# Transformer layer on one core: whole up blocks in 512-column matmuls, h2 and x in tiles of 4 KB, and row sums issued inside the u stage

## The chip, the cores and the metric

One core of a Trainium2 chip runs the whole layer in one launch. The core has five engines with queues of their own: TensorE (matmuls; PE in the profile, its weight loads PEld), VectorE (DVE), ScalarE (ACT), GpSimd (POOL) and SyncE (SP, which issues most transfers). The metric is device time in microseconds (us), lower is better.

## The reference, cut to what matters

```python
S, D, DFF = 512, 1024, 2816          # tokens, model width, FFN width; all float32
h = rmsnorm(x, g_pre_mix)
q, k, v, g, u, sv, a_ret, a_sgu = split(h @ w_in)
y_ret = (layernorm(retention(q, k, v)) * silu(g)) @ w_ret_o      # both directions
u  = gelu(u)
sv = layernorm(gelu(sv))
mixed = einsum('gpq,bnqgc->bnpgc', w_spatial, sv_chunks) + b_spatial
y_sgu = (u * mixed) @ w_sgu_o
x  = x + rmsnorm((sigmoid(a_ret) * y_ret + sigmoid(a_sgu) * y_sgu) @ w_out, g_post_mix)
h2 = rmsnorm(x, g_pre_ffn)
hid = conv3(h2 @ w_up, conv_w) + conv_b     # depthwise, over the tokens
a, b = split(hid)
out = x + rmsnorm((gelu(a) * b) @ w_down, g_post_ffn)
```

## The kernel before

**Arithmetic.** Each float32 operand is kept as a high and a low part (`h2h`/`h2l`, `xh`/`xl`, `wh`/`wl`, in the type float32r). A product is three matmuls into the same PSUM tile: high x high, high x low, low x high. `mm3` (L217 to L220) issues the three. The operand that is loaded into the array (128x128, "weights" for TensorE) and the one that moves through it, 256 or 512 columns wide, are named in the profile after the arrow.

**Weights.** They come as 512 KB units in the order of a list. `w_get` hands out the next unit and, up to a few units ahead, has SyncE load raw tiles, ScalarE copy the high part (L79) and VectorE subtract for the low part (L86, `wl`, `wf`, `dl`).

**Products.** Many are done by a scheme of seven block products in place of eight (Strassen's kind). `Pair` does it for two output blocks of 128 features by all tokens, as seven products of 12 matmuls (L672) on halves of 256 tokens, T0 and T1: 48 matmuls in `part1`, 12 in `part2`, 24 in `part3`. A Pair's `part3` is issued later, behind the next Pair's `part1` or inside another block. Blocks that are not done in pairs are whole blocks: 8 pieces k of the model width by three matmuls each.

**Stages, in the time of the profiled span.** q and k up to 49 us; the retention's scores and states with groups of 512-column products between them (L480 to L482) up to 214; transposes of its result (L605) and the mixing's row sums (L722); u in four Pairs and the gates' first `part1`, 384 narrow matmuls, 217 to 263; the gates, with Pairs, blocks of 512 columns (`f_block`) and the spatial mixing (L745), to 430; the product with w_out (L820 to L822), the norms and the transposes of h2 (`turn`, L883), to 474; the up product to 709.7; the FFN's down product (`products` L1050, `add_whole` L1066), conversions of the result and the end.

**The up product.** 44 blocks, in pairs i of 22 that belong to one output of the gated convolution. The first 4 blocks (EARLY) go in halves of 256 tokens, interleaved with `turn`. i = 2 and 3 are 4 whole blocks; i = 4 to 19 are 8 couples, each a `Pair` on 2 blocks and 2 whole blocks, with the last Pair's `part3` issued inside a whole block; i = 20 and 21 are 4 whole blocks. `up_block` runs the 24 matmuls of T0, then what `between` gives, then those of T1. As a block is done, `conv`, `gated` and `down_forms` turn it into operands of the down product, on ScalarE and VectorE.

**Tiles.** h2 lies in tiles of 2 KB to a partition: for each half of the tokens and each two of the eight pieces k, one. `blk` is a pool of NBLK = 76 such tiles from which nearly all operands come, those of x (`xh`, `xl`, one for each k) and of the down product (`fh`, `fl`) too. The framework orders instructions by their dependences and keeps each engine's order as the code issues it; a tile is taken again when its last reader is done.

**Row sums.** `rw`, `ones` x `wst`, is one float32 product of 512 columns, which the trace shows as two passes (L722). ScalarE copies it to `rws`, which `mix` reads at L745's stage.

Of the kernel before, what the change touches and what calls it, by code (L numbers as in the profile page):

```python
# [10 lines left out]
F32 = mybir.dt.float32  # L11
F32R = mybir.dt.float32r
# [3 lines left out]
P = 128  # L16
D = 1024
S = 512
NT = S // P
KD = D // P  # L20
# [6 lines left out]
NW = 146  # L27
U0, GATE0, GATE1 = 32, 40, 72
LOOK = 4
NBLK = 76  # L30
WARM = 18
RES_OUT = 6
DOWN0 = NW - NF
DP = 9
WHOLE = NF - 2 * DP
EAGER = 7
# [11 lines left out]
def tile_block(ctx: ExitStack, tc, xT, x, wall, par, cs, wsp, bsp, gpost, gpre, gffn, out):  # L48
    nc = tc.nc
    sb = ctx.enter_context(tc.tile_pool(name="sb", bufs=1))  # L50
# [5 lines left out]
    def nm(s):  # L56
        uid[0] += 1
        return f"{s}_{uid[0]}"

    def blk(dt=F32, n="blk", shape=(P, S)):  # L60
        return sb.tile(list(shape), dt, tag="blk", bufs=NBLK, name=nm(n))

    def tmp(n="tmp", shape=(P, S)):
        return sb.tile(list(shape), F32, tag="tmp", bufs=6, name=nm(n))
# [7 lines left out]
    def ps(shape=(P, S)):  # L72
        return pp.tile(list(shape), F32, tag="ps", name=nm("ps"))

    def const(n, shape):
        return sb.tile(list(shape), F32, tag=n, bufs=1, name=n)

    def copy(o, i):
        nc.scalar.activation(out=o, in_=i, func=AF.Copy)  # L79

    def as32(t):
        return t.bitcast(F32)

    def split(hi, lo, src):
        copy(hi, src)
        nc.vector.tensor_sub(lo, src, as32(hi))  # L86
# [7 lines left out]
    i = 0  # L94
    while i < NW:
# [7 lines left out]
        elif i == UP0 + 2 * COUPLES[0][0]:  # L103
# [3 lines left out]
            i = UP0 + 2 * COUPLES[-1][1] + 2  # L107
        elif i == DOWN0:
            for _ in range(2):
                pairs = [[("q", i + j), ("t", i + j)] for j in range(DP)]  # L110
                whole = [[("blk", i + DP)], [("blk", i + DP + 1)]]
# [86 lines left out]
    def w_size(u):  # L198
        return 2 if u[0] in ("blk", "q", "t") else 1

    def w_next():
        u = units[w_pos[1]]
        w_ready[w_pos[1]] = w_unit(u)
        w_pos[1] += 1
        return w_size(u)

    def w_get(look=LOOK):

        i = w_pos[0]
        w_pos[0] += 1  # L210
        room = 2 * look + (2 if w_size(units[i]) == 2 else 0)
        n = sum(w_size(u) for u in units[i : w_pos[1]])
        while w_pos[1] < len(units) and (w_pos[1] <= i or n + w_size(units[w_pos[1]]) <= max(room, 9 if look == LOOK else 0)):
            n += w_next()
        return w_ready.pop(i)

    def mm3(o, ah, al, bh, bl, start, stop):  # L217
        nc.tensor.matmul(o, ah, bh, start=start, stop=False)  # L218
        nc.tensor.matmul(o, ah, bl, start=False, stop=False)  # L219
        nc.tensor.matmul(o, al, bh, start=False, stop=stop)  # L220
# [14 lines left out]
    def col(i):  # L235
        return part[:, i : i + 1]

    xh, xl, xg = [], [], {}

    def load_x(k):  # L240
        t = tmp("xT")
        nc.sync.dma_start(t, xT[k])
        h_, l_ = blk(F32R, "xh"), blk(F32R, "xl")
        nc.scalar.activation(out=h_, in_=t, func=AF.Copy, scale=col(PRE + k))
        xh.append(h_)
        xl.append(l_)
        return t
# [19 lines left out]
    for k in range(KD):  # L267
# [6 lines left out]
        wh, wl = w_get(1 if k < 4 else LOOK)  # L274
# [38 lines left out]
    ones = const("ones", [P, P])  # L313
    nc.gpsimd.memset(ones, 1.0)
    wst = blk(n="wst")
# [49 lines left out]
    raw = []  # L365
    for m in range(8):
        t = blk(n="qkraw")
# [8 lines left out]
    for t in range(NT):  # L376
# [4 lines left out]
            start=True,  # L381
            stop=True,
# [249 lines left out]
    for n, acc in enumerate(t_group()):  # L632
        if n < 2:
            for k in (n + 2, n + 6):
                t = tmp("xT")
# [82 lines left out]
    nc.sync.dma_start(wst, wsp)  # L718
    bst = blk(n="bst")
    nc.gpsimd.dma_start(bst, bsp.rearrange("g p -> (g p)")[None, :].to_broadcast([P, S]))  # L720
    rw = ps()
    nc.tensor.matmul(rw, ones, wst, start=True, stop=True)  # L722
    rws = blk(n="rws")
    copy(rws, rw)
    uT, late = [], None
    for j in range(KD // 2):
        p = Pair(AF.Gelu_apprx_tanh, lambda: blk(n="u"), scale=rbc)
        p.part1()
        if late:
            late.part3()  # L730
        p.part2()
        late = p
        uT += p.t
# [45 lines left out]
    for j in range(KD // 2):  # L779
        for o, t in gated_pair(ogh, ogl, late if j == 0 else None):  # L780
            b = blk(n="r")
# [14 lines left out]
    def bcast(src, n):  # L796
        t = halves(n)
        for i in range(2):
            nc.gpsimd.dma_start(t[i], src[None, i * S : (i + 1) * S].to_broadcast([P, S]))
        return t  # L800
# [32 lines left out]
    def row_scale(q):  # L833
# [7 lines left out]


    gpm, gpf = bcast(gpost, "gpm"), bcast(gpre, "gpr")
    h2h, h2l, h2r = ([[blk(dt, n) for _ in range(4)] for _ in range(2)]
                     for dt, n in ((F32R, "h2h"), (F32R, "h2l"), (F32, "h2r")))
    x1 = [[dp_.tile([P, S], F32, tag=f"x1_{t}{n}", name=f"x1_{t}{n}") for n in range(2)] for t in range(NT)]

    def norms(t, acc):
# [24 lines left out]
            zs.append(z)  # L873
        return zs

    two = "p (i n) -> p i n"

    def turn(t, zs):
        g, c = t // 2, slice((t % 2) * P, (t % 2 + 1) * P)
        for n in range(2):  # L880
            p = ps()
            for f in range(4):
                nc.tensor.transpose(p[:, f * P : (f + 1) * P], zs[n][:, f * P : (f + 1) * P], ident)  # L883
            for i in range(2):
                hi, lo, raw = (h[g][2 * n + i].rearrange(two, i=2)[:, :, c] for h in (h2h, h2l, h2r))
                pf = p[:, 2 * i * P : 2 * (i + 1) * P].rearrange(two, i=2)
                copy(hi, pf)
                copy(raw, pf)
                v.tensor_sub(lo, pf, as32(hi))  # L889

    def h2(k, t):
        f = slice((k % 2) * 256, (k % 2 + 1) * 256)
        g = t.start // 256
        return h2h[g][k // 2][:, f], h2l[g][k // 2][:, f]

    h2forms = {n: [None] * 4 for n in ("S1", "S2", "S3", "S4")}

# [17 lines left out]
    def h2_block(w, o, q):  # L915
        wh, wl = w
        for k in range(KD):
            c = slice(k * P, (k + 1) * P)
            mm3(o[:, q], wh[:, c], wl[:, c], *h2(k, q), k == 0, k == KD - 1)

    def up_block(between=None):
        w, o = w_get(), ps()
        h2_block(w, o, T0)
        if between:
            between()
        h2_block(w, o, T1)
        return o

    early_w, early_o = [], []
# [25 lines left out]
    gp, dforms = [], []  # L955
# [18 lines left out]
        gp.append(blk(n="gp"))  # L974
        v.tensor_mul(gp[-1], ca, cb)  # L975

    def two_parts(t):
        h_, l_ = blk(F32R, "fh"), blk(F32R, "fl")
        split(h_, l_, t)
        return h_, l_  # L980

    def down_forms(j):

        a, b = gp[2 * j], gp[2 * j + 1]
        first = blk(F32R, "fa")
        split(first[:, T0], first[:, T1], a[:, T0])
        s_ = blk(n="fs")
        v.tensor_sub(s_[:, T0], a[:, T1], b[:, T1])
        v.tensor_sub(s_[:, T1], s_[:, T0], a[:, T0])
        v.tensor_sub(a[:, T0], a[:, T0], a[:, T1])  # L990
        v.tensor_add(a[:, T1], b[:, T0], s_[:, T1])
        bh, bl = two_parts(b)
        sh, sl = two_parts(s_)
        th, tl = two_parts(a)
        dforms.append({
            "A11": (first[:, T0], first[:, T1]), "A12": (bh[:, T0], bl[:, T0]), "A22": (bh[:, T1], bl[:, T1]),
            "S1": (sh[:, T0], sl[:, T0]), "S2": (sh[:, T1], sl[:, T1]),
            "S3": (th[:, T0], tl[:, T0]), "S4": (th[:, T1], tl[:, T1]),
        })
# [10 lines left out]
    i = 0  # L1010
    while i < NF:
        if i in couples:
            p = Pair(None, lambda: tmp("c"), h2, h2forms)
            p.part1()
            o = [up_block()]
# [5 lines left out]
        else:  # L1021
            o = []
# [13 lines left out]
    whole = []  # L1036

    def products(m, j, steps={}):
        for n, (unit, at, act) in enumerate(UNITS):
            if n in (0, 3):  # L1040
                wh, wl = w_get()
            if j == 0:
                m[n] = ps()
            f = slice(at * 256, (at + 1) * 256)
            ah, al = dforms[j][act]
            for t in range(2):
                c = slice(t * P, (t + 1) * P)
                o = m[n][:, t * 256 : (t + 1) * 256]
                for i, (a_, w_) in enumerate(((ah, wh), (ah, wl), (al, wh))):
                    nc.tensor.matmul(  # L1050
                        o, a_[:, c], w_[:, f], start=j == t == i == 0,
                        stop=j == DP - 1 and i == 2 and n not in (M2, M3, M4), skip_group_check=True,
                    )
            steps.get(n, lambda: None)()
# [38 lines left out]
        M4: lambda: v.tensor_add(c21, m[M4], e1),  # L1093
    }
    for j in range(DP):
        if j < WHOLE:
            whole.append(two_parts(gp[2 * DP + j]))
        if j % 2 and late:
            down_forms(late.pop(0))
        products(m, j, steps if j == DP - 1 else {})  # L1100
        if j in (3, 5):
            w = w_get()
            for t in range(NT):
                add_whole(m, t, j // 2 - 1, w, j == 5)
            if j == 5:
                copy(c22, m[M8])
# [33 lines left out]
    for t in (0, 2, 1, 3):  # L1140
# [6 lines left out]
        for i, (b, e) in enumerate((((M2, e1), (M3, xx)), ((M4, uu), (M8, yy)))[t // 2]):  # L1147
            f = slice((t % 2) * 256, (t % 2 + 1) * 256)
# [134 lines left out]
```

## Time and profile before

| | |
|---|---|
| median of 3 runs | 832.83 us (831.78 to 833.0) |
| the profiled execution | 833.83 us, of which its span is 832.1 us |
| TensorE | 820.3 us busy, 5728 matmuls |
| VectorE | 660.1 us, 1076 instructions |
| ScalarE | 428.8 us, 729 instructions |
| GpSimd | 100.2 us, 104 instructions |
| granted TensorE clock, mean | 0.996 |
| DMA | 113 GB/s over the span |

The span is from the first to the last instruction that the profiler recorded; the rest of an execution's time lies around it. Busy times of engines overlap. A matmul's own time (some 279 ns at 256 columns, 391 at 512) is longer than the distance from its start to the next one's start, since several are in the array's pipeline at once.

### The profile page before, as it was taken

How to read it: one execution, taken by the hardware profiler on the slowest of the kernel's cores; microseconds unless marked ns; L12 is line 12 of the kernel's file. 1: busy time of each engine (PE TensorE's matmuls, PEld its weight loads, DVE VectorE, ACT ScalarE, POOL GpSimd, SP SyncE). 2: the span in 40 equal slices, each digit the busy share in tenths (PEclk: the TensorE clock that was granted, in tenths of full speed). 3: DMA queues.
4: the chain of work that ended last, by engine and by line, in shares of the span. 5: the costliest groups of instructions: out<-in, count | busy, mean ns of one | idle time of the engine just before them, and what ended most of it. 6: DMA issues, size and time to landing. Idle time of an engine off the chain costs nothing. (4 is left out here: it accounts for less than half of the span.)

```text
span 832.1 us, 14355 instructions
## 1 busy us (share of the span) xinstructions
PE 820.3 (99%) x5728; PEld 762.0 (92%) x5728; DVE 660.1 (79%) x1076; ACT 428.8 (52%) x729; POOL 100.2 (12%) x104
## 2 busy tenths in 40 slices
PE   9999999999999999999999999999999999999995
PEld 7888888888899999999988899999999999999995
DVE  7489898877898787767765679679899789997956
ACT  6635445545665444444444456456666566644431
POOL 0010000102221111133221201111111100000001
PEclk9999999999999999999999999999999999999998
DMA  8733222213233333233458121333333341243344
GB/s 291 245 115 102 76 77 77 76 52 100 72 98 126 102 102 102 80 98 102 130 173 330 51 76 31 109 105 92 124 96 93 116 145 35 81 136 114 103 127 153
DMA packets 29380, 93.84 MB, mean 113 GB/s; under 512 B 3392, under 2 KB 4032, under 8 KB 29312
## 3 DMA queue, kind: packets, MB, share of 16 engines
q1 hardware_dynamic: 26928, 86.85, 32.5%
q0 software_dynamic: 1520, 4.98, 1.8%
q10 hardware_dynamic: 864, 1.09, 0.4%
q8 instruction: 45, 0.74, 0.4%
q14 instruction: 23, 0.19, 0.1%
HBM read 88.71 MB, written 4.19 MB: 112 GB/s over the span
## 5 line engine op out<-in xcount | busy, mean ns | idle before, releaser
L86 DVE TENSOR_TENSOR wl<-raw,wh 128x1024 fp32r<-128x1024 f32 (+1 forms) x93 | 110.6, 1198 | 53.7 <-PE ps L672 27.3
L79 ACT ACTIVATE wf<-raw 128x512 fp32r<-128x512 f32 x140 | 85.3, 626 | 102.4 <-PE ps L219 37.5
L86 DVE TENSOR_TENSOR wf<-raw,wf 128x512 fp32r<-128x512 f32 x140 | 108.0, 787 | 26.6 <-ACT wf L79 25.7
L219 PE MATMUL ps<-h2l,wh 128*128 128x256 f32 x448 | 124.6, 279 | 0.2 <-DVE h2l L889 0.2
L218 PE MATMUL ps<-h2h,wh 128*128 128x256 f32 x448 | 123.7, 278 | 0.0
L220 PE MATMUL ps<-h2h,wl 128*128 128x256 f32 x448 | 123.7, 277 | 0.0
L672 PE MATMUL ps<-sh,wf 128*128 128x256 f32 x640 | 120.1, 277 | 0.1
L79 ACT ACTIVATE wh<-raw 128x1024 fp32r<-128x1024 f32 (+2 forms) x95 | 93.1, 990 | 36.4 <-DMA raw<-wall 12.8
L672 PEld LDWEIGHTS ps<-sh,wf 128*128 128x128 f32 x640 | 101.4, 188 | 0.8 <-DVE c L700 0.3
L672 PE MATMUL ps<-sl,wf 128*128 128x256 f32 x320 | 89.1, 278 | 0.0
L219 PEld LDWEIGHTS ps<-h2l,wh 128*128 128x128 f32 x448 | 83.9, 187 | 0.7 <-DVE h2l L889 0.7
L218 PEld LDWEIGHTS ps<-h2h,wh 128*128 128x128 f32 x448 | 83.8, 188 | 0.3 <-ACT h2h L79 0.3
L220 PEld LDWEIGHTS ps<-h2h,wl 128*128 128x128 f32 x448 | 83.9, 188 | 0.0
L480 PE MATMUL ps<-wh,xh 128*128 128x512 f32 x192 | 75.0, 391 | 0.0
L481 PE MATMUL ps<-wl,xh 128*128 128x512 f32 x192 | 74.9, 390 | 0.0
L482 PE MATMUL ps<-wh,xl 128*128 128x512 f32 x192 | 74.8, 390 | 0.0
L167 POOL TENSOR_TENSOR raw<-raw,raw 128x512 f32<-128x512 f32 x20 | 35.1, 1757 | 238.9 <-DVE raw L165 212.6
L1050 PE MATMUL ps<-dh,fh 128*128 128x256 f32 x216 | 60.9, 282 | 0.2 <-DVE yy L1085 0.2
L1050 PE MATMUL ps<-dh,fl 128*128 128x256 f32 x216 | 60.9, 282 | 0.0
L672 PEld LDWEIGHTS ps<-sl,wf 128*128 128x128 f32 x320 | 60.0, 188 | 0.3
L1050 PE MATMUL ps<-dl,fh 128*128 128x256 f32 x216 | 60.3, 279 | 0.0
L672 PE MATMUL ps<-xh,wf 128*128 128x256 f32 x288 | 54.4, 279 | 0.0
(304 smaller groups left out, 2036.4 us busy)
## 6 DMA issues: line engine op xcount, KB each, us to landing
raw<-wall SPq DMA_DIRECT2D x145, 512.0 KB, 3.5
x<-x SPq DMA_DIRECT2D x24, 256.0 KB, 5.9
xT<-xT SPq DMA_DIRECT2D x8, 256.0 KB, 5.1
x<-x POOLq DMA_DIRECT2D x8, 256.0 KB, 2.3
xT<-xT POOLq DMA_DIRECT2D x4, 256.0 KB, 4.1
out<-zg SPq DMA_DIRECT2D x4, 256.0 KB, 2.6
out<-zs ACTq DMA_DIRECT2D x3, 256.0 KB, 4.3
cs<-cs SPq DMA_DIRECT2D x2, 256.0 KB, 4.0
```

Source lines behind the costliest of these rows:

```text
L79: nc.scalar.activation(out=o, in_=i, func=AF.Copy)
L86: nc.vector.tensor_sub(lo, src, as32(hi))
L167: nc.gpsimd.tensor_tensor(out=w_raw["T2"], in0=w_raw["T1"], in1=w_raw["B22"], op=ALU.add)
L218: nc.tensor.matmul(o, ah, bh, start=start, stop=False)
L219: nc.tensor.matmul(o, ah, bl, start=False, stop=False)
L220: nc.tensor.matmul(o, al, bh, start=False, stop=stop)
L480: nc.tensor.matmul(acc[t], xh[k][:, c], wh[:, f], start=k == 0, stop=False)
L481: nc.tensor.matmul(acc[t], xh[k][:, c], wl[:, f], start=False, stop=False)
L482: nc.tensor.matmul(acc[t], xl[k][:, c], wh[:, f], start=False, stop=k == KD - 1)
L672: nc.tensor.matmul(o, w_[:, c], a_, start=first and k == n == 0, stop=k == 3 and n == 2, skip_group_check=True,)
L1050: nc.tensor.matmul(o, a_[:, c], w_[:, f], start=j == t == i == 0, stop=j == DP - 1 and i == 2 and n not in (M2, M3, M4), skip_group_check= ...
```

## The change

Three edits in one:

1. `up_block` takes both halves of the tokens in one matmul of 512 columns (24 for a block instead of 48). The moving operand is two pieces of 256 columns, 2 KB apart in the 4 KB tile. `between` stands ahead of k = 4, in the middle of the block. The early blocks stay at 256 columns.
2. `h2h` and `h2l` lie in 4 KB tiles (`two`, 8 of them) that hold both halves of the tokens for two pieces k; `xh` and `xl` take the same 8 tiles earlier, two pieces k to a tile. NBLK falls from 76 to 60. The forms of the down product from j = 7 on, and `whole[2]` and `whole[3]`, take such tiles as h2's come free; `whole.append` stands behind `down_forms`.
3. The row sums are issued in `row_sums()`, behind `part1` of the first u Pair.

```diff
-NBLK = 76
+NBLK = 60
...
+    def two(dt=F32R, n="two"):
+        return sb.tile([P, 2 * S], dt, tag="two", bufs=8, name=nm(n))
...
-        h_, l_ = blk(F32R, "xh"), blk(F32R, "xl")
+        if k % 2 == 0:
+            xp2.append((two(n="xh"), two(n="xl")))
+        h_, l_ = (a[:, k % 2 * S : (k % 2 + 1) * S] for a in xp2[-1])
...
-    rw = ps()
-    nc.tensor.matmul(rw, ones, wst, start=True, stop=True)
     rws = blk(n="rws")
-    copy(rws, rw)
+
+    def row_sums():
+        rw = ps()
+        nc.tensor.matmul(rw, ones, wst, start=True, stop=True)
+        copy(rws, rw)
+
...
         p.part1()
         if late:
             late.part3()
+        else:
+            row_sums()
         p.part2()
...
-    h2h, h2l, h2r = ([[blk(dt, n) for _ in range(4)] for _ in range(2)]
-                     for dt, n in ((F32R, "h2h"), (F32R, "h2l"), (F32, "h2r")))
+    four = "p (g i n) -> p g i n"
+    h2h, h2l = ([two(n=n).rearrange(four, g=2, i=2) for _ in range(4)] for n in ("h2h", "h2l"))
+    h2r = [[blk(n="h2r") for _ in range(4)] for _ in range(2)]
...
     def up_block(between=None):
-        w, o = w_get(), ps()
-        h2_block(w, o, T0)
-        if between:
-            between()
-        h2_block(w, o, T1)
+        (wh, wl), o = w_get(), ps()
+        for k in range(KD):
+            if between and k == KD // 2:
+                between()
+            c = slice(k * P, (k + 1) * P)
+            ah, al = (h[k // 2][:, :, k % 2] for h in (h2h, h2l))
+            mm3(o.rearrange("p (g n) -> p g n", g=2), wh[:, c], wl[:, c], ah, al, k == 0, k == KD - 1)
         return o
...
-    def two_parts(t):
-        h_, l_ = blk(F32R, "fh"), blk(F32R, "fl")
+    def two_parts(t, wide=False):
+        if wide:
+            w = two(n="fw")
+            h_, l_ = w[:, :S], w[:, S:]
+        else:
+            h_, l_ = blk(F32R, "fh"), blk(F32R, "fl")
         split(h_, l_, t)
...
-        bh, bl = two_parts(b)
-        sh, sl = two_parts(s_)
-        th, tl = two_parts(a)
+        bh, bl = two_parts(b, j >= EAGER)
+        sh, sl = two_parts(s_, j >= EAGER)
+        th, tl = two_parts(a, j >= EAGER)
...
-        if j < WHOLE:
-            whole.append(two_parts(gp[2 * DP + j]))
         if j % 2 and late:
             down_forms(late.pop(0))
+        if j < WHOLE:
+            whole.append(two_parts(gp[2 * DP + j], j > 1))
```

The changed file is some lines longer, so L672 of before is L677 after, L605 is L610, L722 is L730, L218 to L220 are L221 to L223, L1050 is L1064, and L86 is L89.

On TensorE, at the border from the scores to the u stage, before (`o` is the retention's result, `wst` the spatial weights, `xh`, `xl` the parts of x, `wf` a weight form):

```order
L605 MATMUL ps_2132<-ident,o_1519 128x128
L722 MATMUL ps_2144<-wst_431,ones 128x512
L605 MATMUL ps_2105<-ident,o_1524 128x128
L605 MATMUL ps_2114<-ident,o_1524 128x128
L605 MATMUL ps_2123<-ident,o_1524 128x128
L605 MATMUL ps_2132<-ident,o_1524 128x128
L672 MATMUL ps_2150<-xh_101,wf_1914 128x256
```

and after, at the same border and 45 narrow matmuls later (`sh`, `sl` are the parts of a sum of x blocks):

```order
L610 MATMUL ps_2124<-ident,o_1511 128x128
L677 MATMUL ps_2139<-xh_101,wf_1906 128x256
L677 MATMUL ps_2139<-xl_102,wf_1906 128x256
L677 MATMUL ps_2139<-xh_101,wf_1906 128x256
L610 MATMUL ps_2097<-ident,o_1516 128x128
...
L677 MATMUL ps_2139<-sl_2005,wf_1964 128x256
L677 MATMUL ps_2139<-sh_2004,wf_1964 128x256
L730 MATMUL ps_2210<-wst_423,ones 128x512
L677 MATMUL ps_2139<-sh_465,wf_2012 128x256
```

The row sums have moved from among the transposes to behind the first 48 narrow matmuls of u, and three of those stand ahead of the last four transposes.

On TensorE, at the border from the up product to the down product, before (`ps_7797` is the last up block; `fa`, `fh` are operands of the down product, `dh`, `dl` its weights):

```order
L218 MATMUL ps_7797<-h2h_4390,wh_7470 128x256
L219 MATMUL ps_7797<-h2l_4398,wh_7470 128x256
L220 MATMUL ps_7797<-h2h_4390,wl_7471 128x256
L1050 MATMUL ps_7896<-dh_7593,fa_5952 128x256
L1050 MATMUL ps_7896<-dl_7594,fa_5952 128x256
```

and after:

```order
L221 MATMUL ps_7229<-h2h_4378,wh_6998 128x512
L222 MATMUL ps_7229<-h2l_4382,wh_6998 128x512
L223 MATMUL ps_7229<-h2h_4378,wl_6999 128x512
L1064 MATMUL ps_7304<-dh_7097,fa_5744 128x256
L1064 MATMUL ps_7304<-dl_7098,fa_5744 128x256
```

The last 108 matmuls of the up product are 512 columns wide; the down product behind them has kept its 256.

On VectorE, at the start of the down product, before (`gp` is a gated block, `fs` a sum for a form, `fl` a low part):

```order
L975 TENSOR_TENSOR gp_7855<-cv_7846,cv_7850 128x512
L86 TENSOR_TENSOR fa_7857<-gp_6753,fa_7857 128x256
L988 TENSOR_TENSOR fs_7860<-gp_6753,gp_6764 128x256
L86 TENSOR_TENSOR dl_7922<-raw_7917,dh_7921 128x1024
L989 TENSOR_TENSOR fs_7860<-fs_7860,gp_6753 128x256
```

and after:

```order
L985 TENSOR_TENSOR gp_7263<-cv_7254,cv_7258 128x512
L89 TENSOR_TENSOR fa_7265<-gp_6401,fa_7265 128x256
L1002 TENSOR_TENSOR fs_7268<-gp_6401,gp_6412 128x256
L191 TENSOR_TENSOR raw_7325<-raw_7325,raw_7298 128x256
L1003 TENSOR_TENSOR fs_7268<-fs_7268,gp_6401 128x256
...
L89 TENSOR_TENSOR fw_7369<-gp_6642,fw_7369 128x512
L89 TENSOR_TENSOR fl_7282<-gp_6401,fh_7281 128x512
L187 TENSOR_TENSOR raw_7406<-raw_7382 128x512
L89 TENSOR_TENSOR dl_7330<-raw_7325,dh_7329 128x1024
```

The low part of one weight (`dl_7922` before, `dl_7330` after), which stood three rows behind the last gated block, now stands thirteen rows behind it, after the forms made from two earlier gated blocks. The next low part of that size (`dl_8006`, `dl_7411`) stands at the same place of the queue in both.

More of the change, by code (lines that the diff above doesn't have):

```diff
@@ L236, in col @@
         return part[:, i : i + 1]
-    xh, xl, xg = [], [], {}
+    xh, xl, xp2, xg = [], [], [], {}
     def load_x(k):
@@ L874, in norms @@
         return zs
-    two = "p (i n) -> p i n"
     def turn(t, zs):
@@ L884, in turn @@
             for i in range(2):
-                hi, lo, raw = (h[g][2 * n + i].rearrange(two, i=2)[:, :, c] for h in (h2h, h2l, h2r))
-                pf = p[:, 2 * i * P : 2 * (i + 1) * P].rearrange(two, i=2)
+                hi, lo = (h[2 * n + i][:, g, :, c] for h in (h2h, h2l))
+                raw = h2r[g][2 * n + i].rearrange("p (i n) -> p i n", i=2)[:, :, c]
+                pf = p[:, 2 * i * P : 2 * (i + 1) * P].rearrange("p (i n) -> p i n", i=2)
                 copy(hi, pf)
@@ L891, in h2 @@
     def h2(k, t):
-        f = slice((k % 2) * 256, (k % 2 + 1) * 256)
-        g = t.start // 256
-        return h2h[g][k // 2][:, f], h2l[g][k // 2][:, f]
+        return tuple(h[k // 2][:, t.start // 256, k % 2] for h in (h2h, h2l))
     h2forms = {n: [None] * 4 for n in ("S1", "S2", "S3", "S4")}
```

## The prediction

> **What bounds the kernel now.** I read the head of the page first, then its groups of matmuls, then a table of TensorE's windows by stage, then the timeline at the borders between stages.
>
> ```profile
> span 832.1 us, 14355 instructions
> PE 820.3 (99%) x5728; PEld 762.0 (92%) x5728; DVE 660.1 (79%) x1076; ACT 428.8 (52%) x729; POOL 100.2 (12%) x104
> L219 PE MATMUL ps<-h2l,wh 128*128 128x256 f32 x448 | 124.6, 279 | 0.2 <-DVE h2l L889 0.2
> L480 PE MATMUL ps<-wh,xh 128*128 128x512 f32 x192 | 75.0, 391 | 0.0
> ```
>
> TensorE is busy for 99% of the span, so the end is set by how fast its matmuls follow each other. The 279 and 391 ns of one matmul don't tell that, because matmuls overlap: the pitch from start to start is needed. I take it from long windows, as time divided by count; the count of a window also takes in the two matmuls that were running at its start (279 ns of life against a pitch under 120), so I subtract 2.
>
> ```profile
> core 0: us, PE busy (x), PEclk, DMA share, GB/s
> 20.00:44.00 24.00, 24.00 (x108) 1.00 0.71 246
> 224.00:263.00 39.00, 39.00 (x331) 1.00 0.38 122
> 492.00:637.00 145.00, 145.00 (x1281) 1.00 0.32 99
> 642.00:709.00 67.00, 67.00 (x566) 1.00 0.32 96
> 710.00:768.00 58.00, 58.00 (x495) 1.00 0.35 107
> ```
>
> The first window holds 512-column matmuls: 24.00/106 = 226.4 ns. The other four hold 256-column ones, and all are wholly busy at a granted clock of 1.00, yet they differ: 145/1279 = **113.4 ns** in the first part of the up product, but 39/329 = **118.5** in the u stage, 67/564 = **118.8** in the last part of the up product, and 58/493 = **117.6** in the FFN's down product. The same lines, on tiles of the same form, run at 113.4 before 637 and at 118.8 after 642. So a train of narrow matmuls has a quick and a slow pitch, and what it reads doesn't decide which. The timeline shows where the one turns into the other.
>
> ```profile
> 639.34 0.28 PE L672 MATMUL ps<-h2h,wf 128*128 128x256 f32 x1
> 639.73 0.39 PE L672 MATMUL ps<-sh,wf 128*128 128x256 f32 x1
> 639.95 0.28 PE L672 MATMUL ps<-sl,wf 128*128 128x256 f32 x1
> 214.71 1.31 PE L605 MATMUL ps<-ident,o 128*128 128x128 f32 x10 [0.27 <-DVE o L615]
> 215.86 1.02 PE L722 MATMUL ps<-wst,ones 128*128 128x512 f32 x2
> 216.72 0.60 PE L605 MATMUL ps<-ident,o 128*128 128x128 f32 x4
> 217.07 0.36 PE L672 MATMUL ps<-xh,wf 128*128 128x256 f32 x1
> ```
>
> Into the slow pitch it went at a wait (639.34 to 639.73 is 390 ns instead of 113) and after the 128-column transposes ahead of 217.07. Out of it, it went at 263, where the gates begin and 512-column matmuls come between:
>
> ```profile
> 263.07 0.40 PE L218 MATMUL ps<-gh,wh 128*128 128x512 f32 x1
> 263.31 0.40 PE L219 MATMUL ps<-gl,wh 128*128 128x512 f32 x1
> 263.54 0.40 PE L220 MATMUL ps<-gh,wl 128*128 128x512 f32 x1
> 265.39 0.39 PE L219 MATMUL ps<-gl,wh 128*128 128x512 f32 x1
> 265.61 0.39 PE L220 MATMUL ps<-gh,wl 128*128 128x512 f32 x1
> 268.56 0.28 PE L672 MATMUL ps<-sh,wf 128*128 128x256 f32 x1
> 269.93 0.40 PE L218 MATMUL ps<-gh,wh 128*128 128x512 f32 x1
> 272.67 0.28 PE L672 MATMUL ps<-xh,wf 128*128 128x256 f32 x1
> 275.40 0.40 PE L218 MATMUL ps<-gh,wh 128*128 128x512 f32 x1
> ```
>
> The first wide ones are 240 and 230 ns apart, from 265.39 on it is 220 to 227; and the narrow trains behind them, 12 from 268.56 to 269.93 (114.2 ns each) and 24 from 272.67 to 275.40 (113.8), are quick. My reading: a wide train ends the slow pitch, and the narrow train behind it starts quick.
>
> **The change part by part.**
>
> *Whole up blocks 512 wide.* 1152 matmuls of 256 columns become 576 of 512. At the quick pitch that is worth next to nothing: 2 x 113.4 - 226.4 = 0.4 ns a pair, 576 x 0.4 = 0.2 us. Every change of width costs something: in the rows above 12 wide ones from 269.93 to 272.67 took 2.74 us, 0.02 more than 12 x 226.4, and the 12 narrow ones before them 0.01 more than 12 x 113.4. A couple now has three wide stretches between narrow ones, as the gates have; 8 couples x 3 x 0.03 = +0.7 us.
>
> The gain is in the slow stretch. The tail of the up product, from 639.73 to the last row here, had the slow pitch throughout:
>
> ```profile
> 709.61 0.28 PE L220 MATMUL ps<-h2h,wl 128*128 128x256 f32 x1
> 709.73 0.28 PE L1050 MATMUL ps<-dh,fa 128*128 128x256 f32 x1
> ```
>
> 70.0 us at 118.8 ns are 589 matmuls; at 113.4 they take 5.4 ns less each, **-3.2 us**. Here wide and narrow alternate, and the last four blocks are all wide. The one wide operand is no run of 512 columns but two of 256, 2 KB apart. No matmul of the trace reads so. From below I bound it by the contiguous 512-column one at 226.4 ns; from above by two narrow ones at the slow pitch, 2 x 118.8 = 237.6, since a seam that costs a narrow matmul's whole turn is the furthest row I have. I take 226.4, the row that it is nearest to: as many columns, weights of the same 128x128. The upper end would cost 576 x 11.2 = 6.5 us, and stands among the rivals.
>
> [...]
>
> *Row sums inside u.*
>
> ```profile
> 279.82 0.28 PE L745 MATMUL ps<-wst,sv 128*128 128x128 f32 x1
> 279.85 0.36 PE L672 MATMUL ps<-xh,wf 128*128 128x256 f32 x1
> 285.39 0.40 PE L218 MATMUL ps<-gh,wh 128*128 128x512 f32 x1
> ```
>
> The two f32 passes of L722 (215.86 to 216.72, 0.86 us) aren't removed; they are issued 48 matmuls later, behind the first Pair's part1. ScalarE's copy of their result is wanted only by the first mix (L745, at 279), so nothing waits for it. But 512-column passes now stand inside the slow u train, and by the reading above the rest, 384 - 48 = 336 matmuls, runs at 113.4 instead of 118.5: **-1.7 us**. That two f32 passes suffice is the weakest step, since at 263 it took some ten wide fp32r matmuls until the pitch was steady. For it speaks that the f32 mix matmuls of L745, 128 columns wide, stand ahead of a narrow train of 48 that takes 5.54 us with its start (115.4 each); against it that the transposes, also 128 wide, stand ahead of a slow one.
>
> *Into the down product.* It starts with narrow matmuls only. Behind the wide last blocks it should start quick, and stay so to its first wait. VectorE is short there:
>
> ```profile
> core 0: us, PE busy (x) PEld busy (x) DVE busy (x) ACT busy (x) POOL busy (x), PEclk, DMA share, GB/s
> 690.00:735.00 45.00, 45.00 (x383) 45.00 (x382) 44.78 (x81) 27.02 (x42) 0.00 (x0) 1.00 0.24 71
> 725.18 1.23 DVE L86 TENSOR_TENSOR dl<-raw,dh 128x1024 fp32r<-128x1024 f32 x1
> ```
>
> It has 0.2 us idle in 45. Its low part dl of 725.18 lands at 726.41, and TensorE reads it first with the 142nd matmul of L1050, at 709.73 + 141 x 0.1176 = 726.3: just in time. A quicker start wants it 141 x 4.2 ns = 0.6 us sooner, and the quicker up tail since 690 (20 us x 4.5%) another 0.9 sooner, while VectorE, which has the same work ahead of it to within 0.7 us by the order of the changed kernel, can't come sooner. So a wait of 0 to 2.0 us arises; I take 0.8, which eats the quick start's -0.6. And a wait, as at 639, sends the train back into the slow pitch, so the 804 matmuls behind stay at 117.6. Sum of this part: +0.2.
>
> *Edits at nothing.* Part3 of a Pair now falls between k = 3 and 4 of a block instead of between its halves: the same matmuls on other PSUM banks. h2 and x in tiles of 4 KB: NBLK falls from 76 to 60 as 8 tiles of twice the size come in, the same bytes; ScalarE and VectorE write the same elements. Five or so late forms for the down product now wait for h2 tiles to come free, the first at the last block's k = 1, about 4 us before that product starts; they are read only from its 164th matmul on (19 us later), and that distance hides the wait. If it were gone, VectorE's next low parts would slip by as much, in the same just-in-time place.
>
> Sum: -3.2 + 0.7 - 1.7 + 0.2 = -4.0 us, and about -0.1 for the wait at 639.34 of which half may go: -4.1. The profiled execution took 833.83 us, 1.73 outside its span of 832.1; the median of the runs is 832.83, 1.0 less. So 833.83 - 4.1 - 1.0 = **828.7 us**.
>
> **The rivals.**
>
> *A. Also the down product stays quick.* For it: the sooner it wants dl, the more depends on VectorE's order, and the wait may be under what tips the pitch. Then 360 matmuls up to 768 (58 us less the first 141) gain 4.2 ns each, 1.5 us, and all 804 at most 3.4: 827.2 to 825.3, say 826.3.
>
> *B. The row sums don't end the slow pitch in u* (two passes are too few). Everything else as forecast: 828.7 + 1.7 = 830.4.
>
> *C. It doesn't do what it seems to: the slow pitch belongs to the place, or comes back.* For it: the tail has some wait in it whatever the width, and VectorE at 0.2 us idle in 45 may pace it; then only 0.2 us of count is saved against 0.7 of width changes, 833.3. Against it: between 642 and 709 TensorE was busy for all 67.00 us. [...]
>
> *D. Slower: the seam of the two-piece operand costs.* It decides from (4.1 + 1.7)/576 = 10 ns for each wide matmul, beyond which the kernel is slower by more than 0.2%. At 20 ns, which is what a change of width costs in the rows above, it is 576 x 0.020 = 11.5 us dearer: 828.7 + 11.5 = 840.2. For it: no row shows such an operand. Against it: a narrow train is itself a new operand every 113.4 ns, and 2 x 113.4 is only 0.4 over a wide one, so a fresh start alone costs next to nothing.
>
> **How the numbers follow.** The forecast 0.33, A 0.27, B 0.16, C 0.14, D 0.10. 0.2% of 832.83 is 1.7 us, about what a measurement of this kernel can tell from no change. Faster are the forecast, A and B: 0.76. C is the same, 0.14. D is slower, 0.10. The likeliest one's own range, with the wait of 0 to 2.0 in place of 0.8 and half the u term open, is 827.9 to 830.7; the range takes in A down to 824.6 (its full 3.4 us, with a wait of none) and B and the better half of C up to 832.4, which leaves out D, the worse half of C and a little below.
>
> **What would show it.** In the changed profile: 512-column up matmuls at 226 to 228 ns start to start (234 or more means D); a window 645 to 700 whose narrow stretches count 113 to 114 ns; u at 113.4 behind the row sums (118.5 means B); the first 140 matmuls of the down product at 113.4, then a wait for dl of 0 to 2 us, then 117.6 (all at 113.4 means A). TensorE still at 99%, with 576 matmuls fewer. The forecast fails if the slow pitch stands in the wide stretches too (over 230 ns with no wait), or if the waits in the up tail grow to over 4 us.

## The result, and the profile after

The changed kernel takes 836.39 us (median of 5 runs, 835.16 to 837.64) where the kernel before takes 833.0 on the same chip: a ratio of **1.0041, 95% interval 1.0028 to 1.0054**. It is slower, by about 3.4 us, and the forecast was 4 us faster. The profiled execution took 836.42 us.

From its page: the span, TensorE's line, and one of the three groups of up matmuls (192 wide and 64 narrow ones in one group).

```profile
span 834.6 us, 13213 instructions
PE 822.8 (99%) x5152; PEld 738.6 (88%) x5152; DVE 657.3 (79%) x1076; ACT 429.0 (51%) x729; POOL 99.6 (12%) x104
L222 PE MATMUL ps<-h2l,wh 128*128 128x512 f32 (+1 forms) x256 | 93.5, 367 | 0.2 <-DVE h2l L899 0.2
```

There are 576 matmuls fewer, as forecast, and TensorE is as full as before. So the pitch must have become worse. From TensorE's timeline of the changed kernel, the border into the first couple's whole block, the start of the second couple, and the last 108 wide matmuls up to the down product:

```profile
520.27 0.28 PE L677 MATMUL ps<-h2h,wf 128*128 128x256 f32 x1
...
525.72 0.39 PE L221 MATMUL ps<-h2h,wh 128*128 128x512 f32 x1
525.95 0.40 PE L222 MATMUL ps<-h2l,wh 128*128 128x512 f32 x1
526.19 0.39 PE L223 MATMUL ps<-h2h,wl 128*128 128x512 f32 x1
526.42 0.40 PE L221 MATMUL ps<-h2h,wh 128*128 128x512 f32 x1
...
541.20 0.28 PE L677 MATMUL ps<-h2h,wf 128*128 128x256 f32 x1
...
546.91 0.40 PE L221 MATMUL ps<-h2h,wh 128*128 128x512 f32 x1
...
686.71 0.40 PE L221 MATMUL ps<-h2h,wh 128*128 128x512 f32 x1
...
711.67 0.40 PE L223 MATMUL ps<-h2h,wl 128*128 128x512 f32 x1
711.91 0.28 PE L1064 MATMUL ps<-dh,fa 128*128 128x256 f32 x1
```

The same places before:

```profile
521.07 0.28 PE L672 MATMUL ps<-h2h,wf 128*128 128x256 f32 x1
541.47 0.28 PE L672 MATMUL ps<-h2h,wf 128*128 128x256 f32 x1
684.05 0.28 PE L218 MATMUL ps<-h2h,wh 128*128 128x256 f32 x1
```

From 520.27 to 525.72 the 48 narrow matmuls of the Pair take 5.45 us, 113.5 ns each: quick. No wait follows; but the wide ones behind them come at 230, 240 and 230 ns, and in the couples it stays so: the last 108 take 25.20 us, **233.3 ns** each, where I had put 226.4. The couples, up to these last four and a half blocks, take 686.71 - 520.27 = 166.44 us, before 684.05 - 521.07 = 162.98: **+3.5 us** where -1.3 was forecast (373 of the 589 slow ones lie there, -2.0, and +0.7). The narrow ones have become slow with the wide ones: the 48 of the second couple's first part take 5.71 us, 541.20 to 546.91, 119.0 ns each, while the whole first couple before (541.47 - 521.07 = 20.40 us for 180) stood at 113.3. In the last four and a half blocks, which were slow before (216 narrow ones from 684.05 to 709.73, 25.68 us), the wide ones are 0.5 us shorter, where 1.2 was forecast. One stretch of wide ones stood in between. Of the first four wide blocks (i = 2 and 3) 95 matmuls are in the trace (one of the 96 is missing), from this row to 520.27, at 228.8 ns each, and the narrow ones behind them are the 48 quick ones above:

```profile
498.53 0.39 PE L222 MATMUL ps<-h2l,wh 128*128 128x512 f32 x1
```

Around the up product little changed: the down product and the end take 834.6 - 711.91 = 122.7 us, before 832.1 - 709.73 = 122.4.

The u stage stayed slow. The windows of the changed kernel, with the count less 2 as above, give 38.00/320 = 118.75 ns:

```profile
core 0: us, PE busy (x), PEclk, DMA share, GB/s
224.00:262.00 38.00, 38.00 (x322) 1.00 0.39 125
```

### The profile page after: what moved, and what is told of

The parts are those of the page before. It is cut to its first block, busy times and chain, and to the rows that moved or that the text cites. A ratio compares the mean times of both kernels' runs of the same rounds, so it can differ in the third digit from the quotient of the medians.

```text
span 834.6 us, 13213 instructions
## 1 busy us (share of the span) xinstructions
PE 822.8 (99%) x5152; PEld 738.6 (88%) x5152; DVE 657.3 (79%) x1076; ACT 429.0 (51%) x729; POOL 99.6 (12%) x104
## 4 chain that ended last, share of the span: by engine, by line
PE 93%; DVE 3%; issue 1%; ACT 1%; POOL 1%; DMA 0%; DVEq 0%; POOLq 0%; SPq 0%; ACTq 0%
PE ps L677 24%; PE ps L221 12%; PE ps L222 12%; PE ps L223 12%; PE ps L1064 10%; PE ps L485 5%; PE ps L486 5%; PE ps L487 5%; PE ps L1080 2%; PE ps L831 1%; PE ps L830 1%; PE ps L832 1%; PE ps L755 1%; PE ps L285 1%; POOL qr L849 0%
## 5 line engine op out<-in xcount | busy, mean ns | idle before, releaser
L89 DVE TENSOR_TENSOR wl<-raw,wh 128x1024 fp32r<-128x1024 f32 (+1 forms) x93 | 106.9, 1158 | 54.5 <-PE ps L677 37.6
L89 DVE TENSOR_TENSOR wf<-raw,wf 128x512 fp32r<-128x512 f32 x140 | 108.4, 791 | 28.4 <-ACT wf L82 27.5
L677 PE MATMUL ps<-sh,wf 128*128 128x256 f32 x640 | 121.5, 278 | 0.0
L677 PEld LDWEIGHTS ps<-sh,wf 128*128 128x128 f32 x640 | 101.9, 188 | 1.1 <-ACT u L82 0.4
L222 PE MATMUL ps<-h2l,wh 128*128 128x512 f32 (+1 forms) x256 | 93.5, 367 | 0.2 <-DVE h2l L899 0.2
L221 PE MATMUL ps<-h2h,wh 128*128 128x512 f32 (+1 forms) x256 | 93.4, 367 | 0.0
L223 PE MATMUL ps<-h2h,wl 128*128 128x512 f32 (+1 forms) x256 | 92.9, 364 | 0.0
L677 PE MATMUL ps<-sl,wf 128*128 128x256 f32 x320 | 89.7, 280 | 0.0
L677 PEld LDWEIGHTS ps<-sl,wf 128*128 128x128 f32 x320 | 60.0, 187 | 0.7
L223 PEld LDWEIGHTS ps<-h2h,wl 128*128 128x128 f32 x256 | 48.1, 188 | 8.8
L222 PEld LDWEIGHTS ps<-h2l,wh 128*128 128x128 f32 x256 | 48.0, 188 | 7.8 <-DVE h2l L899 0.7
L221 PEld LDWEIGHTS ps<-h2h,wh 128*128 128x128 f32 x256 | 47.7, 188 | 7.8 <-ACT h2h L82 0.3
L677 PE MATMUL ps<-xh,wf 128*128 128x256 f32 x288 | 54.6, 279 | 0.0
L82 ACT ACTIVATE dh<-raw 128x768 fp32r<-128x768 f32 (+1 forms) x36 | 34.0, 949 | 33.7 <-PE ps L1064 21.2
L1064 PE MATMUL ps<-dh,fh 128*128 128x256 f32 x168 | 47.3, 281 | 0.3 <-DVE yy L1099 0.2
L1064 PE MATMUL ps<-dh,fl 128*128 128x256 f32 x168 | 47.3, 281 | 0.0
```

What stands on the lines that cost most here:

```text
L677: nc.tensor.matmul(o, w_[:, c], a_, start=first and k == n == 0, stop=k == 3 and n == 2, skip_group_check=True,)
L1064: nc.tensor.matmul(o, a_[:, c], w_[:, f], start=j == t == i == 0, stop=j == DP - 1 and i == 2 and n not in (M2, M3, M4), skip_group_check= ...
```

## The experiments

Four theories for the wide pitch were on the table: the seam between the operand's two pieces (S), the change of widths or the couples' traffic (R), the place of h2 in its 4 KB tiles (L), and, after the first three runs, an offset between addresses (O). The diffs show the lines that matter.

### e1_run_of_512: no seam

```diff
-    four = "p (g i n) -> p g i n"
+    four = "p (i g n) -> p i g n"
-            ah, al = (h[k // 2][:, :, k % 2] for h in (h2h, h2l))
-            mm3(o.rearrange("p (g n) -> p g n", g=2), wh[:, c], wl[:, c], ah, al, ...)
+            ah, al = (h[k // 2][:, k % 2].rearrange("p g n -> p (g n)") for h in (h2h, h2l))
+            mm3(o, wh[:, c], wl[:, c], ah, al, ...)
```

> The changed kernel with one difference: in the 4 KB tiles of h2 the two token halves of a piece k lie side by side, so that the wide up matmul's moving operand is one run of 512 columns instead of two runs of 256 that are 2 KB apart. Theory S (the seam in the moving operand brings the slow pitch and keeps it): the wide up matmuls stand at 226 to 228 ns instead of 233, the narrow ones between them at 113 to 115 instead of 119, the down product starts some 5 us earlier than in the changed kernel, and the time is 829 to 831 us. Theory R (the slow pitch comes by the change of widths or by the traffic in the couples, whatever the operand's shape): 233 and 119 as in the changed kernel, 836 us. Theory L (the place of h2 in the 4 KB tiles): also 836.

Measured: 836.41 us (835.02 to 837.91), ratio to the kernel before 1.0059 [1.0037, 1.0082]. Its timeline, at the first couple and the last 108 wide matmuls:

```profile
520.87 0.28 PE L677 MATMUL ps<-h2h,wf 128*128 128x256 f32 x1
687.30 0.40 PE L221 MATMUL ps<-h2h,wh 128*128 128x512 f32 x1
712.50 0.28 PE L1064 MATMUL ps<-dh,fa 128*128 128x256 f32 x1
```

166.43 us for the couples and 25.20 for the last 108, as with the seam, to a hundredth. The seam costs nothing; S falls.

### e2_narrow_in_4k: the tiles without the wide matmuls

```diff
     def up_block(between=None):
-        (wh, wl), o = w_get(), ps()
-        for k in range(KD):
-            ... (one 512-column mm3 for each k)
+        w, o = w_get(), ps()
+        h2_block(w, o, T0)
+        if between:
+            between()
+        h2_block(w, o, T1)
```

> The changed kernel with its tiles, but with the up blocks as before: 24 narrow matmuls on T0, then 24 on T1. Theory S (seam): no seam, so the up product runs as in the kernel before, at 113.4 ns up to some wait and 118.8 behind it; 831 to 834 us. Theory L (the place of h2 in the 4 KB tiles makes the slow pitch): 118 to 119 ns from the first couple on, 838 us or more. Theory R (change of widths): as the kernel before, 833.

Measured: 830.93 us, ratio 0.9988 [0.9972, 1.0004]. TensorE's windows in u and in the first part of the up product (columns as in the window above), and the last 216 narrow up matmuls:

```profile
224.00:246.00 22.00, 22.00 (x197) 1.00 0.33 114
492.00:630.00 138.00, 138.00 (x1220) 1.00 0.31 100
```

```profile
681.52 0.28 PE L221 MATMUL ps<-h2h,wh 128*128 128x256 f32 x1
707.20 0.28 PE L1062 MATMUL ps<-dh,fa 128*128 128x256 f32 x1
```

The up product is that of the kernel before: 138/1218 = 113.3 ns, then 25.68 us for the last 216. The 4 KB tiles, the pools and the moved forms cost the up product nothing, so L falls too, and the loss belongs to the width itself. But u is quick here (22/195 = 112.8, which one matmul more or less in the count makes 112.2 to 113.4), with the same order of u as in the changed kernel, where it was slow.

### e3_rows_only: the row sums alone

```diff
+        else:
+            row_sums()       # in the kernel before, nothing else changed
```

> The kernel before with the row sums alone moved into the u stage. My forecast gave 1.7 us for it; the changed kernel's trace shows u still at 118 ns behind the row sums, so I now expect u at 118.5 and 832.5 to 833.5 us, no difference. If the row sums' place matters in another way (the transposes' order), up to 1 us sooner at the gates' start.

Measured: 831.3 us, ratio 0.9999 [0.9982, 1.0015]: no difference. Its windows in u:

```profile
224.00:246.00 22.00, 22.00 (x196) 1.00 0.35 113
248.00:260.00 12.00, 12.00 (x104) 1.00 0.44 157
```

Quick first (22/194 = 113.4), slow after 248 (12/102 = 117.6), in one stage of one run.

### What was left: an address

512-column matmuls of the gates take 227.9 ns (24 in the 5.47 us from 285.39 before), and most of those of the up product 233.3, with a moving operand of two pieces or of one (e1). I compared what else differs between them and found it in the code that places weights in their slots:

```python
hi, lo = (slot("wh", 16), slot("wl", 48)) if i >= DOWN0 else (
    (slot("wh", 48), slot("wl", 16)) if i >= UP0 else (slot("wh"), slot("wl"))
)
```

The second argument is a start within the slot, in words of 4 bytes. Slots and tiles start at the same address modulo 128 bytes. So the weights of q, k, the scores' groups, the gates' blocks and w_out lie at distance 0 from the moving operand (modulo 128), those of the up and down products, and the Pairs' forms, at distance 64. (In the scores' groups, w_out and the down product the weights are the operand that moves, and the other one is loaded into the array; the distance is the same either way.) In the kernel before, **every 512-column matmul had distance 0, and every 256-column one distance 64**, save the retention's narrow ones and the warm-up's. The change made the up matmuls wide and left their weights at 64. That is theory O.

### e4_wide_offset0: the changed kernel with the weights moved by 64 bytes

```diff
-                (slot("wh", 48), slot("wl", 16)) if i >= UP0 else (slot("wh"), slot("wl"))
+                (slot("wh", 48), slot("wl", 16)) if UP0 <= i < UP0 + EARLY else (slot("wh"), slot("wl"))
```

> The changed kernel with one difference: the weights of the 24 whole up blocks stand at the start of their slots, as those of the gates' blocks do, so that weights and moving operand of the wide up matmuls have the same address modulo 128 bytes, as in every other wide matmul of the kernel; in the changed kernel they are 64 bytes apart, as for all its narrow matmuls. Theory O (a 512-column matmul wants an offset of 0, a 256-column one an offset of 64; with the other offset it costs some 6 ns more and throws the trains behind it into the slow pitch): wide up matmuls at 226 to 228 ns, narrow ones between them at 113 to 115, the down product's start 5 us sooner than in the changed kernel, 828 to 830 us on a chip where the kernel before takes 831.5 to 833. Theory R (the change of widths or the couples' traffic makes the slow pitch): 233 and 119, 836 us.

Measured: 830.61 us (12 runs, 828.82 to 830.86), ratio to the kernel before **0.9987 [0.9976, 0.9998]**. The first couple, the last 108 wide matmuls, and the down product's start:

```profile
518.54 0.28 PE L677 MATMUL ps<-h2h,wf 128*128 128x256 f32 x1
539.04 0.28 PE L677 MATMUL ps<-h2h,wf 128*128 128x256 f32 x1
544.48 0.40 PE L221 MATMUL ps<-h2h,wh 128*128 128x512 f32 x1
679.79 0.40 PE L221 MATMUL ps<-h2h,wh 128*128 128x512 f32 x1
704.30 0.28 PE L1064 MATMUL ps<-dh,fa 128*128 128x256 f32 x1
```

The last 108 take 24.51 us: **226.9 ns**, with the two-piece operand. The first couple takes 20.50 us, 0.10 over the 20.40 of a quick narrow couple: three stretches of wide ones, as forecast 0.09; the 48 narrow ones behind it (539.04 to 544.48) are quick, 113.3 ns. The couples, up to these last blocks, take 161.25 us, 5.2 less than in the changed kernel, and no slow pitch arises in the tail. One offset of 64 bytes is the whole loss of the up product. R falls. The time itself was expected at 828 to 830 us against 831.5 to 833, and came out at 830.61 against 830.78: the kernel before was quicker beside this run than expected.

### e5_gates_offset64: the offset where the change did nothing

```diff
-                (slot("wh", 48), slot("wl", 16)) if i >= UP0 else (slot("wh"), slot("wl"))
+                (slot("wh", 48), slot("wl", 16)) if i >= GATE0 else (slot("wh"), slot("wl"))
```

> The kernel before with one difference, far from the change: the weights of the gates' wide blocks (and of a quarter of the product with w_out) stand 64 bytes off the moving operand. Theory O: the gates' wide matmuls go from 226.7 to 229 to 234 ns and the narrow ones between them from 113.4 to 119; 400 wide by 2 to 6.5 ns and some 620 narrow by 5.4 are 4 to 6 us slower. Theory R: the gates' pitch as before, no difference.

Measured: 837.08 us, ratio 1.0071 [1.0046, 1.0096], some 6 us slower. One block of 24 wide matmuls in the gates, from its first to the narrow one behind it (before, the first row is in the prediction at 285.39, the other is below it here):

```profile
285.45 0.40 PE L218 MATMUL ps<-gh,wh 128*128 128x512 f32 x1
291.05 0.28 PE L672 MATMUL ps<-sh,wf 128*128 128x256 f32 x1
```

```profile
290.86 0.28 PE L672 MATMUL ps<-sh,wf 128*128 128x256 f32 x1
```

5.60 us against 5.47: 233.3 ns against 227.9. The gates have taken over the slow pitch of the changed kernel's up product, with contiguous operands and nothing of the change in them; only their first 24 stayed quicker (229.2 ns), as did the 12 narrow ones behind those (114.3), and the other narrow ones between the blocks went to 119, as expected.

The same edit shifts a quarter of w_out's weights, the first 48 matmuls there, and in w_out the weights are the operand that moves. Those 48, from their first to the one behind them, in e5 and before:

```profile
433.39 0.39 PE L820 MATMUL ps<-wh,mh 128*128 128x512 f32 x1
444.49 0.39 PE L820 MATMUL ps<-wh,mh 128*128 128x512 f32 x1
```

```profile
428.85 0.39 PE L820 MATMUL ps<-wh,mh 128*128 128x512 f32 x1
439.73 0.39 PE L820 MATMUL ps<-wh,mh 128*128 128x512 f32 x1
```

11.10 us against 10.88: 231.2 ns against 226.7, with the loaded operand where it was; the 24 behind them, unshifted again, are at 227.5. So it isn't the loaded operand's own place alone that counts.

The up product of e5 is that of the kernel before, and its tail was quick this time. The last 216 narrow up matmuls, which took 25.68 us there, take 24.48, 113.3 ns each, though a wait stands ahead of them here too (at 644.45):

```profile
686.74 0.28 PE L218 MATMUL ps<-h2h,wh 128*128 128x256 f32 x1
711.22 0.28 PE L1050 MATMUL ps<-dh,fa 128*128 128x256 f32 x1
```

So a wait doesn't always leave the slow pitch behind it. The u stage shows the same: in e3 it turned slow at a pause of 290 ns between two starts at 246.49, and in e2 it went over one of 356 ns at 246.42 and stayed quick.

### e6_narrow_offset0: the converse

```diff
-                (slot("wh", 48), slot("wl", 16)) if i >= UP0 else (slot("wh"), slot("wl"))
+                (slot("wh", 48), slot("wl", 16)) if UP0 <= i < UP0 + EARLY else (slot("wh"), slot("wl"))
```

This is the edit of e4, made in the kernel before, where the up blocks are narrow.

> The kernel before with its narrow up blocks' weights at offset 0 (the early blocks as they were). Theory O: those 1152 narrow matmuls take about 120 ns, as the retention's narrow ones at offset 0 do, in place of 113.4 to 118.9, and the Pairs' narrow ones between them take the slow pitch from 500 us on; up product 5 to 8 us longer, 837 to 840 us. Theory R: as the kernel before.

Measured: 837.07 us, ratio 1.0068 [1.005, 1.0087]. The last 24 narrow ones of a Pair and the last 216 of the up blocks:

```profile
685.12 0.28 PE L672 MATMUL ps<-h2h,wf 128*128 128x256 f32 x1
687.84 0.28 PE L218 MATMUL ps<-h2h,wh 128*128 128x256 f32 x1
713.76 0.28 PE L1050 MATMUL ps<-dh,fa 128*128 128x256 f32 x1
```

25.92 us: 120.0 ns each, the figure of the forecast. The edit that gains 0.5% with wide matmuls (1.0041 to 0.9987) loses 0.7% with narrow ones. One part of what I expected failed: the Pairs' narrow matmuls between them, at distance 64, stayed at 113.3 ns (24 in 2.72 us, 685.12 to 687.84): the slow pitch of the one doesn't pass to the other here. The down product starts 4.0 us later than in the profile of before (713.76 against 709.73), a little under the 5 to 8 expected.

### e7 to e10: distances of 32 and 96 bytes

```diff
+ (slot("wh", 8), slot("wl", 8)) if i >= UP0 + EARLY      # e7 (changed kernel), e9 (kernel before): 32 bytes
+ (slot("wh", 24), slot("wl", 24)) if i >= UP0 + EARLY    # e8 (changed kernel), e10 (kernel before): 96 bytes
```

> The changed kernel with the whole up blocks' weights 32 bytes off the moving operand (modulo 128), between the 64 that costs and the 0 that doesn't. If the distance counts in steps (same or other half of 128 bytes), the wide pitch is that of one neighbour: 226 to 228 or 229 to 233 ns; if it counts by degrees, about 229 to 230. Theory R, already against e4: 233 whatever the offset.

> As e7_wide_offset32 with 96 bytes: if the sign of the distance doesn't matter, the pitch is that of e7_wide_offset32; if 96 acts as 64 bytes do, 233 ns.

> The kernel before with its narrow whole up blocks at 32 bytes. At 64 they were 113.4 (quick) or 118.9 (slow), at 0 always 120.0. In steps: one of these; by degrees: 116 to 117.

> As e9_narrow_offset32 with 96 bytes: the same as at 32 if the sign doesn't matter.

The wide blocks' or narrow whole blocks' weights move, both parts alike; the early blocks stay at 64. One run each: 836.47, 835.21, 839.01 and 838.36 us, where the kernel before took 833.26. The last up matmuls (108 wide, or 216 narrow), of e7, e8, e9 and e10 in turn:

```profile
686.70 0.39 PE L221 MATMUL ps<-h2h,wh 128*128 128x512 f32 x1
711.90 0.28 PE L1064 MATMUL ps<-dh,fa 128*128 128x256 f32 x1
```

```profile
685.32 0.40 PE L221 MATMUL ps<-h2h,wh 128*128 128x512 f32 x1
710.63 0.28 PE L1064 MATMUL ps<-dh,fa 128*128 128x256 f32 x1
```

```profile
689.31 0.28 PE L218 MATMUL ps<-h2h,wh 128*128 128x256 f32 x1
714.86 0.28 PE L1050 MATMUL ps<-dh,fa 128*128 128x256 f32 x1
```

```profile
689.00 0.28 PE L218 MATMUL ps<-h2h,wh 128*128 128x256 f32 x1
714.34 0.28 PE L1050 MATMUL ps<-dh,fa 128*128 128x256 f32 x1
```

| distance, modulo 128 bytes | 512 columns, ns | 256 columns, ns |
|---|---|---|
| 0 | **226.9** (e4) | 120.0 (e6) |
| 32 | 233.3 (e7) | 118.3 (e9) |
| 64 | 233.3 (changed kernel, e1), 228.8 in their first four blocks | **113.3** (e2, before its wait) or 118.9 (behind it); 113.3 behind a wait too in e5 |
| 96 | 234.4 (e8) | 117.3 (e10) |

Each width has one distance of the four at which it is quickest, and not the same one. At 32 bytes the wide ones cost as much as in the slow stretches at 64, so their cost doesn't grow by degrees. Each of e7 to e10 is a single run.

## Why the prediction was wrong

**The pitch as the bound, and the two pitches.** Held. TensorE is busy for 99% of the span before and after (820.3 us of 832.1, 822.8 of 834.6), and all that I found to move the time by more than a microsecond was a pitch.

**"I take 226.4, the row that it is nearest to: as many columns, weights of the same 128x128."** This is the step that failed. I bounded the wide up matmul from below by rows of the same width and looked at the moving operand's shape, where nothing was to be found, and not at the weights' place, where the row and the new matmul differed. All wide rows had distance 0, all quick narrow ones 64, so the trace of before could not show a wide one at 64; but that width and distance went together in its rows was to be read from the code. At 233.3, where 480 of the 576 stood, the term costs 6.9 ns a matmul, and at the 228.8 of the other 96 it costs 2.4: some 3.5 us in place of nothing. That is under the upper bound (237.6), but I treated that end as the price of a seam. The span was to come out at 832.1 - 4.1 = 828.0 us and was 834.6. Of these 6.6 us, 5.5 lie between the first couple and the down product: 711.91 - 520.27 = 191.64 us, before 188.66, so +3.0 where -2.5 was forecast (-3.2 + 0.7).

**"A wide train ends the slow pitch."** At distance 0 it did at the gates' start, before and after: u's narrow ones from 250 us on stood at 118.9 ns, the 12 behind the first 24 wide ones at 113.9. At 64 it can begin it: in the changed kernel quick narrow matmuls (113.5 ns) go into the wide ones at 525.72, the second couple's narrow ones take 119.0, and no wait is needed for the slow pitch to stay. The same kind of border at 498.53 gave 228.8 ns and a quick train behind; what decides between the two is open. The slow pitch took the -3.2 away, and gave the quick couples a loss that they hadn't had. With the distance mended the term is right against this profile of before: from the first couple to the down product e4 takes 704.30 - 518.54 = 185.76 us, before 709.73 - 521.07 = 188.66, so -2.9, where -2.5 was forecast.

**Count.** At 0.4 ns a pair I put it at 0.2 us. In the quick pitch that holds (2 x 113.3 against 226.9). In the slow pitch two narrow ones cost 237.8 and a wide one 233.3, so a wide one saves 4.5 ns there: the 0.5 us of the last blocks.

**Row sums in u, -1.7.** Not so: 118.75 in the changed kernel, and e3 alone moved no time. The sums don't end the slow pitch; in windows of six kernels with the sums inside u it was slow in three (118.75 ns in the changed kernel, 22/186 = 118.3 in e7, 22/185 = 118.9 in e8), quick in two (112.8 in e2 and e4) and half and half in one (113.4, then 117.6, in e3); in three with the sums ahead of u it was slow (118.5 before, 118.9 in e9 and e10). What decides is open, and nine profiles, one of each kernel, don't tell whether the moved sums change the odds.

**Into the down product, +0.2.** The sum held by luck (+0.3), its parts did not. The wait for `dl` came where it was put, and was short. From the changed kernel's list of waits, and VectorE's timeline:

```profile
PE ps L1064 <- DVE dl L89: 0.2, 1, 0.2
```

```profile
727.91 1.23 DVE L89 TENSOR_TENSOR dl<-raw,dh 128x1024 fp32r<-128x1024 f32 x1
```

0.2 us by the list, for 0 to 2.0 forecast. But the quick start of -0.6 isn't there, not even in e4, whose wide matmuls run at 226.9 up to the border: its down product and end take 827.0 - 704.30 = 122.7 us, before 122.4. So rival A (the down product quick throughout) had no footing. That product's 756 matmuls of `products` stood at 117.8 ns before and 117.6 after, their waits apart, at neither pitch of the up product's narrow matmuls (113.3 and 118.9), although it has 256 columns and distance 64 as they do. Why is open.

**Edits at nothing.** Nothing speaks against it: e2 has them all, at a ratio of 0.9988 [0.9972, 1.0004], and with the up product of before; but its u stage was quick in the profile, which a small cost elsewhere could hide behind.

**The rivals.** B's part came true (u slow). C, that the slow pitch comes back, is what one sees, but its reason, traffic or the place, is not the cause. D named the right side and the wrong mechanism: it put a cost on the wide matmul, but on its seam, which e1 shows to be free. It also set the threshold at 10 ns a matmul, taking the gains for granted; 6.9 sufficed, since the slow pitch spread to the narrow trains between. The range's upper end, 832.4, puts half of C below it; that was my estimate and no run shows it: C's worked figure is 833.3, and the changed kernel took 836.39.

**What is left of the gain.** e4 beats both kernels, the one before by 0.13% in the ratio (by medians 830.61 against 830.78), though its up product is 2.9 us shorter than in the profile of before. The kernel before ran between 830.04 and 833.7 us beside it; no profile was taken of those runs, so whether its own tail was quick in the shorter ones stays open. That it can be, e5's profile shows. The -3.2 us would then be a gain only where the tail before is slow, and the forecast took it from one profile as if it were there in all.

## What to carry to other kernels

Before pricing a new matmul by an old row, compare both operands' addresses as well as their shapes: in this kernel's up product each width had its own best distance between weights and moving operand (0 bytes modulo 128 for 512 columns, 64 for 256), and another one cost up to 3% of a wide matmul (234.4 ns against 226.9) and up to 6% of a narrow one (120.0 against 113.3), and in some places slowed the narrow trains behind it (119.0 in the changed kernel). Here the change of width had to take the offset of the weights along: without it the ratio was 1.0041, with it 0.9987 (e4). A constant in the code that nobody explains (a start of 16 or 48 words in a slot) is a thing to understand before the edit, not after it.

## What the runs showed of the hardware

That the address of the weights matters at all I had not expected. With the same data volumes, moving only the weights by 64 bytes changes the wide pitch from 233.3 (changed kernel) to 226.9 ns (e4) and the narrow one from 113.3 or 118.9 (before) to 120.0 (e6). What was measured is the pitch at four places of the loaded operand; why it differs between them no run shows. Is it the distance that counts, or that operand's own place? In e5 the wide matmuls of w_out slowed as the moving operand alone was shifted (231.2 against 226.7), which speaks for the distance. But the down product, where also the moving operand is the shifted one, is at distance 64 and stands at 117.6 in the prediction's window, not at 113.3: the distance alone isn't the whole rule for narrow ones. That it repeats every 128 bytes was not tested.

Whether a train's pitch passes to the next differs: behind the wide ones at 64 that took 233.3 ns the narrow trains were slow without any wait (119.0 ns in the changed kernel), behind those that took 228.8 they were quick (113.5), behind wide ones at 0 they were quick (113.3 in e4), and between narrow ones at 0, which take 120.0, they were quick too (113.3 in e6). In e8, with the wide ones at 96, narrow trains of 48 were quick (113.6) and those of 12 slow (119.0). What sets the state of a train is open.
